# Three small moves in a hybrid decoder layer: where the last hidden blocks come back to, when the queries are copied, and which weights are fetched behind the keys

## The chip, the cores and the metric

The kernel runs on one NeuronCore of a Trainium2 chip. Its engines work side by side and wait for each other by semaphores: TensorE multiplies matrices, VectorE and ScalarE work on whole tiles, GpSimd does a few small things, and SyncE issues nearly all DMA transfers, in the order in which they are written. The metric is the time of one execution on the device in microseconds (us), as a median over runs.

## What is computed

One layer for 256 tokens of width 1024, in float32:

```
h = x + 0.5 * (silu(n1 @ w_gate1) * (n1 @ w_up1)) @ w_down1        n1 = rmsnorm(x), hidden width 2816
n = rmsnorm(h);  z = n @ w_in = q | k | v | u | gv                  each 512 wide
attn = softmax(q k^T / 8, causal) v                                 8 heads of 64; 256 tokens are one block
gm   = gelu(u) * (W_s layernorm(gelu(gv)) + b_s)                    W_s lower triangular, chunks of 128 tokens
g    = sigmoid(n @ w_gate + b_gate)                                 two gates of 1024
h = h + (g[:1024] * (attn @ w_a) + g[1024:] * (gm @ w_g)) @ w_out
h = h + 0.5 * (silu(n3 @ w_gate2) * (n3 @ w_up2)) @ w_down2         n3 = rmsnorm(h)
out = rmsnorm(h)
```

## The kernel before

**Precision.** Every large product is made of three: each float32 operand is split into a high part (a cast, on ScalarE, line 205) and a low part (the difference, on VectorE, line 207), and TensorE adds high x high, high x low and low x high (lines 200 to 202). So each weight goes through SyncE's load, ScalarE's cast and VectorE's subtraction before TensorE may use it.

**Weights.** They come in units of 1 MB, in the order in which TensorE uses them, each loaded as two halves of 512 KB (line 149, tiles `raw`) into a ring of 7 buffers (`RAW`), and split into a ring of 4 units (`w`). A half is loaded as soon as VectorE has finished with the half seven before it, unless `hold[0]` stops the loads at a number of halves. Some places set `hold[0]`, so that transfers of the program's own tiles are not queued behind weights, and set it back to `None` later.

**Order.** TensorE and SyncE run in the order in which the code is written. From the first down product to the gates ScalarE and VectorE do too (`in_order`). Elsewhere a scheduler orders these two.

**Hidden blocks.** The product `silu(g)*u` of a feed-forward layer is made with tokens on the partitions, and the down product wants features there. `glu` transposes 32x32 squares on VectorE into a tile of the ring `hg` (two buffers), `leave` stores it to DRAM (`f1way`, `f2way`), `arrive` fetches it back with the squares rearranged by four DMAs (line 381, tiles `f1back`, `f2back`), and `settle` splits it into the operand (`f1h`, `f2h`). This goes in groups of four blocks of 128 features; the 22 blocks make five groups and a last one of two. `back` is a single buffer, so a fetch waits until the group before it is split. `rest()` lists what remains when the down product begins, to be done after its weight units 1, 2, 3 and so on. The ring `hg` is also used by the transposed tiles of the first down product's output (line 542).

**The middle.** After the first down product come, with the first half of the features and then with the second, the products q, k and gv; then u and v whole, then the gates. q and k are scaled by ScalarE (line 609) and transposed by VectorE (610), stored (723, 725), and fetched back in another shape (727, 730: `qback`, and the keys into `qk`). Before the scores (line 624) the queries' tile is copied once more by ScalarE (line 743). The scores go to six PSUM banks; VectorE adds the causal mask on the way out (line 631), ScalarE copies the rest (630). The spatial product (line 673) needs the layer norm of gv, whose gain and bias (`ln_g`, `ln_b`) are fetched behind the keys (731, 732). All PSUM tiles come from one ring of eight banks, so u's two banks are next used by the spatial product, and the first two score banks by v's product (line 374). `hold[0] = 2 * mv + 2` (line 578) lets the loads run up to the first of v's two weight units until the keys' fetch has been issued (line 733).

Of the kernel before, what the change touches and what calls it, by code (L numbers as in the profile page):

```python
# [10 lines left out]
F32 = mybir.dt.float32  # L11
# [7 lines left out]
P = 128  # L19
D = 1024  # L20
S = 256
# [24 lines left out]
def block_kernel(ctx, tc, t, out):  # L46
    nc = tc.nc
# [5 lines left out]
    tmp = ctx.enter_context(tc.tile_pool(name="tmp", bufs=2))  # L53
# [53 lines left out]
    def add_units(name, n):  # L107
        first = len(units)
        units.extend((name, i) for i in range(n))
        return first  # L110
# [9 lines left out]
    mu, mv = (add_units(name, 2) for name in ("u", "v"))  # L120
    mg = add_units("gate", 8)
# [9 lines left out]
    hold = [None]  # L131
# [72 lines left out]
    def split(hi, lo, src, later=False):  # L204
        nc.scalar.copy(hi, src)  # L205
        def rest():
            nc.vector.tensor_sub(lo, src, hi.bitcast(F32))  # L207
        return rest if later else rest()
# [65 lines left out]
    def down_features(i0, n_units, both_of_k, scale, gain, nT, name, free, near, behind):  # L274
# [41 lines left out]
        for rest in lows:  # L316
            rest()
# [45 lines left out]
    def chunk(i0, nT, name, c, us=range(2), ps=None, apart=1):  # L363

        if ps is None:
            ps = [bank(f"{name}_{c}{j}") for j in range(NT)]
        for u in us:
            w = unit(i0 + 2 * c + apart * u, ALONE)  # L370
            for k in range(4):
                for j in range(NT):
                    st = tuple(p[:, j * P:(j + 1) * P] for p in block_of(nT, 4 * u + k))
                    mm3(ps[j], st, (w[:, k, 0, :], w[:, k, 1, :]), u + k == 0, u == 1 and k == 3)
        return ps

    def from_way(to, way):

        squares32 = way.rearrange("(q r) a n -> r q a n", r=32)
        for a in range(4):  # L380
            nc.sync.dma_start(to[32 * a:32 * a + 32], squares32[:, :, a, :])
# [9 lines left out]
    class Hidden:  # L391
# [28 lines left out]

        def arrive(self, p):
            n = 32 * self.blocks(p)
            self.back[p] = tmp.tile([P, S // 32, n], F32, tag="back", name=f"{self.name}back{p}", bufs=1)
            from_way(self.back[p], self.way.pop(p))

        def settle(self, p):
# [9 lines left out]
        def rest(self):  # L436

            last = NC // 2
            def first():
                self.leave(NC - 1)  # L440
                self.arrive(last - 1)
            return [first, lambda: self.settle(last - 1), lambda: self.arrive(last), lambda: self.settle(last)]


    nT = alloc_T("n1", ("nA", "nB"))
# [86 lines left out]
    with in_order():  # L532
# [25 lines left out]
        last = 2 * FB - 4  # L558
        sums = [None, None]
        for i in range(FB // 2):  # L560
            w = unit(f1d + i, ALONE)
            at = range(4 * i, 4 * i + 4)
            for s, j in [(s, j) for j in range(NT) for s in at] if 4 * i == last else [(s, j) for s in at for j in range(NT)]:
                f, b = divmod(s, FB)
# [10 lines left out]
            if i == FB // 2 - 3:  # L575
                norm_parts(0)

        hold[0] = 2 * mv + 2
        psq = chunk(mq, nT2, "q", 0, [0], apart=3)
        rs2 = []  # L580
        for j in range(NT):
# [124 lines left out]
        def layer_norm(j):  # L706
            st = small.tile([P, 6], F32, tag="st", name=f"st{j}")
            nc.vector.bn_stats(st, gv[:, j, :])
            mvr = small.tile([P, 2], F32, tag="mvr", name=f"mvr{j}")
            nc.vector.bn_aggr(mvr, st)  # L710
            ve = small.tile([P, 1], F32, tag="ve", name=f"ve{j}")
            nc.vector.tensor_scalar(ve, mvr[:, 1:2], EPS, None, op0=ALU.add)
            r = small.tile([P, 1], F32, tag="lnr", name=f"lnr{j}")
            nc.gpsimd.tensor_tensor(r, ve, nhalf, op=ALU.pow)
            nc.vector.scalar_tensor_tensor(gv[:, j, :], gv[:, j, :], mvr[:, 0:1], lng, op0=ALU.subtract, op1=ALU.mult)
            nc.vector.scalar_tensor_tensor(gv[:, j, :], gv[:, j, :], r, lnb, op0=ALU.mult, op1=ALU.add)

        chunk(mq, nT2, "q", 0, [1], psq, 3)  # L720
        turn_qk(0, psq)
        chunk(mk, nT2, "k", 0, [1], psk, 3)
# [3 lines left out]
        q_back = tmp.tile([P, S // 32, P], F32, tag="back", name="qback", bufs=1)  # L726
        from_way(q_back, qk_way[0])
        qk = act.tile([P, 2, 4 * S], F32, tag="nC", name="qk")
# [6 lines left out]
        chunk(mgv, nT2, "gv", 0, [1], psgv, 3)  # L735
        for j in range(NT):
            nc.scalar.activation(gv[:, j, :], psgv[j], AF.Gelu_apprx_tanh, scale=rs2[j])
        for j in range(NT):
            layer_norm(j)
        psu = chunk(mu, nT2, "u", 0, [0])  # L740

        qT = qk[:, 0].rearrange("p (k t) -> p k t", k=4)
        nc.scalar.copy(qT.rearrange("p k (q c) -> p q k c", c=32), q_back.rearrange("p q (k c) -> p q k c", c=32))
        chunk(mu, nT2, "u", 0, [1], psu)
        for j in range(NT):
            nc.scalar.activation(ut[:, j, :], psu[j], AF.Gelu_apprx_tanh, scale=rs2[j])
# [233 lines left out]
```

## Time and profile before

| | |
|---|---|
| Median of three runs | 529.79 us (528.45 to 531.68) |
| Profiled execution | 527.75 us, its span 526.0 us |
| TensorE busy | 515.0 us (98%) |
| VectorE busy | 352.1 us (67%) |
| ScalarE busy | 264.7 us (50%) |
| DMA | 126.82 MB, mean 241 GB/s |
| Chain that ended last | 88% TensorE, 6% DMA, 2% VectorE |

The span is the time from the first to the last instruction of the profiled execution; what lies around it makes the rest of that execution's time. The chain that ended last is followed back from the last instruction, at each step to what released it. In a timeline a row is one instruction, or several alike in a row (x4), with the time it started, how long it ran, and in brackets how long its engine was idle before and what ended that. `SPq` is SyncE issuing DMAs, and the time of such a row is that of the issues, not of the transfers. Times of TensorE's instructions overlap, so its speed is read from the distance between starts.

### The profile page before, as it was taken

The numbers are of one execution on the slowest core, as the hardware profiler recorded it, in microseconds if no ns is written. First come the engines' busy times: TensorE is split into PE (matmuls) and PEld (weight loads), VectorE is DVE, ScalarE is ACT, GpSimd is POOL, SyncE is SP. The second block draws the span as 40 slices with busy tenths as digits, with TensorE's granted clock in tenths as the row PEclk, the third lists the DMA queues.
The fourth block names the chain that finished last, engine by engine and source line by source line (L and its number), as shares of the span: only waits on it lengthen the run. The fifth ranks groups of instructions, "written<-read, shape, count | busy, mean of one in ns | idle before, by whom it ended". The sixth has DMA issues, their size and how long they took to land.

```text
span 526.0 us, 6697 instructions
## 1 busy us (share of the span) xinstructions
PE 515.0 (98%) x2401; PEld 428.4 (81%) x2401; DVE 352.1 (67%) x481; ACT 264.7 (50%) x369; POOL 12.0 (2%) x25
## 2 busy tenths in 40 slices
PE   8999999999989999989999999999999999999995
PEld 6888888888868888878888898888888888888884
DVE  6886666575447565569976787987965755575424
ACT  7755354554434545558655524666444453463402
POOL 0010000000000010000000000001000000000002
PEclk9999999999999999999999999999999999999998
DMA  8998597979767955697799666738697879677302
GB/s 317 372 340 309 152 360 254 251 232 286 192 180 236 316 173 192 156 366 278 187 357 321 241 182 175 299 117 323 209 286 266 277 257 317 190 241 219 140 0 81
DMA packets 63921, 126.82 MB, mean 241 GB/s; under 512 B 11664, under 2 KB 36752, under 8 KB 63760
## 3 DMA queue, kind: packets, MB, share of 16 engines
q1 hardware_dynamic: 63600, 126.06, 74.3%
q8 instruction: 19, 0.31, 0.2%
q10 hardware_dynamic: 288, 0.33, 0.2%
q14 instruction: 14, 0.11, 0.1%
HBM read 113.26 MB, written 13.11 MB: 240 GB/s over the span
## 4 chain that ended last, share of the span: by engine, by line
PE 88%; DMA 6%; DVE 2%; SPq 1%; issue 1%; ACT 1%; POOLq 0%; DVEq 0%; POOL 0%; ACTq 0%
PE f L200 14%; PE f L201 14%; PE f L202 14%; PE acch L202 4%; PE acch L201 4%; PE acch L200 4%; PE acc L174 3%; PE g L201 3%; PE g L202 3%; PE g L200 3%; DMA f1back<-f1way 3%; PE down L202 2%; PE down L200 2%; PE down L201 2%; DMA raw<-in_v 2%; PE acc L179 1%
## 5 line engine op out<-in xcount | busy, mean ns | idle before, releaser
L207 DVE TENSOR_TENSOR w<-raw,w 128x1024 fp32r<-128x1024 f32 x180 | 211.5, 1217 | 77.7 <-ACT w L205 77.6
L205 ACT CAST w<-raw 128x1024 fp32r<-128x1024 f32 x180 | 179.7, 1049 | 103.8 <-PE f L202 48.7
L202 PE MATMUL f<-w,n 128*128 128x512 f32 x336 | 130.7, 389 | 0.0
L200 PE MATMUL f<-w,n 128*128 128x512 f32 x336 | 130.7, 389 | 0.0
L201 PE MATMUL f<-w,n 128*128 128x512 f32 x336 | 130.7, 389 | 0.0
L202 PEld LDWEIGHTS f<-w,n 128*128 128x128 f32 x336 | 63.1, 188 | 13.1
L200 PEld LDWEIGHTS f<-w,n 128*128 128x128 f32 x336 | 63.1, 188 | 13.1
L201 PEld LDWEIGHTS f<-w,n 128*128 128x128 f32 x336 | 63.1, 188 | 13.1
L200 PE MATMUL down<-w,f1h 128*128 128x512 f32 x88 | 34.3, 390 | 1.6 <-ACT f1h L205 1.6
L202 PE MATMUL down<-w,f1h 128*128 128x512 f32 x88 | 34.4, 390 | 0.0
L201 PE MATMUL down<-w,f1h 128*128 128x512 f32 x88 | 34.3, 389 | 0.0
L200 PE MATMUL acch<-w,f2h 128*128 128x512 f32 x84 | 32.7, 389 | 0.0
L201 PE MATMUL acch<-w,f2h 128*128 128x512 f32 x84 | 32.7, 389 | 0.0
L202 PE MATMUL acch<-w,f2h 128*128 128x512 f32 x84 | 32.7, 389 | 0.0
L406 ACT ACTIVATE f2s<-f,rstd 128x256 f32<-128x256 f32 x22 | 10.3, 474 | 29.0 <-PE f L202 28.8
L200 PE MATMUL g<-w,n 128*128 128x512 f32 x64 | 24.9, 389 | 0.0
L201 PE MATMUL g<-w,n 128*128 128x512 f32 x64 | 24.9, 389 | 0.0
L202 PE MATMUL g<-w,n 128*128 128x512 f32 x64 | 24.9, 389 | 0.0
L408 DVE SCALAR_TENSOR_TENSOR f2a<-f,rstd,f2s 128x256 f32<-128x256 f32 x22 | 10.3, 474 | 20.5 <-ACT f2s L406 20.5
L406 ACT ACTIVATE f1s<-f,rstd 128x256 f32<-128x256 f32 x22 | 10.3, 473 | 24.3 <-PE f L202 22.8
L200 PEld LDWEIGHTS down<-w,f1h 128*128 128x128 f32 x88 | 16.5, 188 | 5.4 <-ACT f1h L205 2.0
L202 PEld LDWEIGHTS down<-w,f1h 128*128 128x128 f32 x88 | 16.5, 188 | 3.8 <-DVE f1h L207 0.4
(181 smaller groups left out, 648.8 us busy)
## 6 DMA issues: line engine op xcount, KB each, us to landing
raw<-in_f SPq DMA_DIRECT2D x84, 512.0 KB, 5.9
raw<-in_f1d SPq DMA_DIRECT2D x22, 512.0 KB, 6.2
raw<-in_f2d SPq DMA_DIRECT2D x22, 512.0 KB, 7.0
raw<-in_gate SPq DMA_DIRECT2D x16, 512.0 KB, 6.5
raw<-in_out SPq DMA_DIRECT2D x8, 512.0 KB, 5.4
f1way<-f1t SPq DMA_DIRECT2D x11, 256.0 KB, 6.5
f2way<-f2t SPq DMA_DIRECT2D x11, 256.0 KB, 5.0
front<-in_first SPq DMA_DIRECT2D x7, 384.0 KB, 6.0
```

The source lines that it names most:

```text
L174: nc.tensor.matmul(ps, st, both.rearrange("p two n -> p (two n)"), start=first, stop=last)
L179: nc.tensor.matmul(ps[:, n:], st, both[:, 0, :], start=False, stop=False)
L200: nc.tensor.matmul(ps, sh, mh, start=first, stop=False)
L201: nc.tensor.matmul(ps, sh, ml, start=False, stop=False)
L202: nc.tensor.matmul(ps, sl, mh, start=False, stop=last)
L205: nc.scalar.copy(hi, src)
L207: nc.vector.tensor_sub(lo, src, hi.bitcast(F32))
L406: nc.scalar.activation(sg, ps[j][:, :CH], AF.Silu, scale=rs[j])
L408: nc.vector.scalar_tensor_tensor(a, ps[j][:, CH:], rs[j], sg, op0=ALU.mult, op1=ALU.mult)
```

## The change

Three edits. **First**, a group of two blocks is fetched into a tile of the ring `hg` instead of the single buffer `back`, and `rest()` fetches it in its first step, right behind the group of four before it; splitting it moves up by one step. Since both feed-forward layers use the class, it holds for both. **Second**, the copy of the queries on ScalarE is written ahead of the layer norm and of the u products, and so ahead of the casts of the weights that those ask for. **Third**, `hold[0]` is `2 * mg`, so that both of v's units are loaded before the keys' transfers and only the gates' units behind them.

```diff
--- before.py
+++ after.py
@@ -420,7 +420,9 @@
 
         def arrive(self, p):
             n = 32 * self.blocks(p)
-            self.back[p] = tmp.tile([P, S // 32, n], F32, tag="back", name=f"{self.name}back{p}", bufs=1)
+
+            beside = dict(tag="back", bufs=1) if n == P else dict(tag="hg")
+            self.back[p] = tmp.tile([P, S // 32, n], F32, name=f"{self.name}back{p}", **beside)
             from_way(self.back[p], self.way.pop(p))
 
         def settle(self, p):
@@ -439,7 +441,8 @@
             def first():
                 self.leave(NC - 1)
                 self.arrive(last - 1)
-            return [first, lambda: self.settle(last - 1), lambda: self.arrive(last), lambda: self.settle(last)]
+                self.arrive(last)
+            return [first, lambda: self.settle(last - 1), lambda: self.settle(last)]
 
 
     nT = alloc_T("n1", ("nA", "nB"))
@@ -575,7 +578,7 @@
             if i == FB // 2 - 3:
                 norm_parts(0)
 
-        hold[0] = 2 * mv + 2
+        hold[0] = 2 * mg
         psq = chunk(mq, nT2, "q", 0, [0], apart=3)
         rs2 = []
         for j in range(NT):
@@ -714,7 +717,6 @@
             nc.gpsimd.tensor_tensor(r, ve, nhalf, op=ALU.pow)
             nc.vector.scalar_tensor_tensor(gv[:, j, :], gv[:, j, :], mvr[:, 0:1], lng, op0=ALU.subtract, op1=ALU.mult)
             nc.vector.scalar_tensor_tensor(gv[:, j, :], gv[:, j, :], r, lnb, op0=ALU.mult, op1=ALU.add)
-
 
 
         chunk(mq, nT2, "q", 0, [1], psq, 3)
@@ -735,12 +737,12 @@
         chunk(mgv, nT2, "gv", 0, [1], psgv, 3)
         for j in range(NT):
             nc.scalar.activation(gv[:, j, :], psgv[j], AF.Gelu_apprx_tanh, scale=rs2[j])
+
+        qT = qk[:, 0].rearrange("p (k t) -> p k t", k=4)
+        nc.scalar.copy(qT.rearrange("p k (q c) -> p q k c", c=32), q_back.rearrange("p q (k c) -> p q k c", c=32))
         for j in range(NT):
             layer_norm(j)
         psu = chunk(mu, nT2, "u", 0, [0])
-
-        qT = qk[:, 0].rearrange("p (k t) -> p k t", k=4)
-        nc.scalar.copy(qT.rearrange("p k (q c) -> p q k c", c=32), q_back.rearrange("p q (k c) -> p q k c", c=32))
         chunk(mu, nT2, "u", 0, [1], psu)
         for j in range(NT):
             nc.scalar.activation(ut[:, j, :], psu[j], AF.Gelu_apprx_tanh, scale=rs2[j])
```

SyncE at the start of the first down product (`raw` from `in_f1d` are its weights, `f1way` the stored hidden blocks), before:

```order
L419 DMA f1way_1207<-f1t_1145 128x2x256
L381 DMA f1back_1209<-f1way_1056 32x8x128 x4
L149 DMA raw_1_1217<-in_f1d 128x1024
L149 DMA raw_0_1221<-in_f1d 128x1024
L149 DMA raw_1_1252<-in_f1d 128x1024
L149 DMA raw_0_1256<-in_f1d 128x1024
L381 DMA f1back_1282<-f1way_1207 32x8x64 x4
```

and now:

```order
L419 DMA f1way_1207<-f1t_1145 128x2x256
L381 DMA f1back_1209<-f1way_1056 32x8x128 x4
L381 DMA f1back_1214<-f1way_1207 32x8x64 x4
L149 DMA raw_1_1222<-in_f1d 128x1024
L149 DMA raw_0_1226<-in_f1d 128x1024
L149 DMA raw_1_1257<-in_f1d 128x1024
L149 DMA raw_0_1261<-in_f1d 128x1024
```

The fetch of the last two blocks (32x8x64) stands directly behind that of the four before, and ahead of four weight halves instead of behind them.

ScalarE from the activation of gv on (`w_1876` and `w_1877` are v's second unit, `w_1910` is the first of the gates), before:

```order
L737 ACT_TABLE_LOAD
L737 ACTIVATE mixed<-gv_1689,rstd_1642 128x512
L737 ACTIVATE mixed<-gv_1690,rstd_1644 128x512
L205 CAST w_1876<-raw_0_1809 128x2x512
L205 CAST w_1876<-raw_1_1811 128x2x512
L743 COPY qk<-qback 128x8x4x32
L205 CAST w_1910<-raw_0_1813 128x2x512
L205 CAST w_1910<-raw_1_1815 128x2x512
```

and now:

```order
L739 ACT_TABLE_LOAD
L739 ACTIVATE mixed<-gv_1689,rstd_1642 128x512
L739 ACTIVATE mixed<-gv_1690,rstd_1644 128x512
L742 COPY qk<-qback 128x8x4x32
L205 CAST w_1877<-raw_0_1698 128x2x512
L205 CAST w_1877<-raw_1_1734 128x2x512
L205 CAST w_1910<-raw_0_1813 128x2x512
L205 CAST w_1910<-raw_1_1815 128x2x512
```

The copy has moved ahead of the two casts of v's second unit. Behind these rows both have the activation of u and the copies of the scores.

SyncE around the transposed queries and keys (`qkway` is where they are stored), before:

```order
L149 DMA raw_1_1694<-in_v 128x1024
L723 DMA qkway_1727<-mixed 128x2x512
L725 DMA qkway_1728<-mixed 128x2x512
L381 DMA qback<-qkway_1727 32x8x128 x4
L381 DMA qk<-qkway_1728 32x8x128 x4
L731 DMA mixed<-in_ln_g 128x512
L732 DMA mixed<-in_ln_b 128x512
L149 DMA raw_0_1809<-in_v 128x1024
L149 DMA raw_1_1811<-in_v 128x1024
L149 DMA raw_0_1813<-in_gate 128x1024
```

and now:

```order
L149 DMA raw_1_1694<-in_v 128x1024
L149 DMA raw_0_1698<-in_v 128x1024
L149 DMA raw_1_1734<-in_v 128x1024
L725 DMA qkway_1729<-mixed 128x2x512
L727 DMA qkway_1730<-mixed 128x2x512
L381 DMA qback<-qkway_1729 32x8x128 x4
L381 DMA qk<-qkway_1730 32x8x128 x4
L733 DMA mixed<-in_ln_g 128x512
L734 DMA mixed<-in_ln_b 128x512
L149 DMA raw_0_1813<-in_gate 128x1024
```

Both halves of v's second unit have moved from behind `ln_b` to ahead of the queries' store. VectorE's order in the middle is the same before and now: subtractions of v's first unit, layer norm, subtractions of v's second unit and of the gates' first, mask additions.

## Rows read from the trace of the kernel before

**Rows 1.** Waits of TensorE (line waiting, releaser, us in total, times, longest).

```profile
PE sc L624 <- ACT qk L743: 1.7, 1, 1.7
PE down L200 <- ACT f1h L205: 1.6, 1, 1.6
```

**Rows 2.** Timeline of TensorE around the first stop (start us, us, instruction, idle before).

```profile
151.28 0.39 PE L200 MATMUL down<-w,f1h 128*128 128x512 f32 x1
...
152.41 0.39 PE L202 MATMUL down<-w,f1h 128*128 128x512 f32 x1
154.40 0.50 PE L200 MATMUL down<-w,f1h 128*128 128x512 f32 x1 [1.60 <-ACT f1h L205]
...
158.00 0.39 PE L202 MATMUL down<-w,f1h 128*128 128x512 f32 x1
```

**Rows 3.** Timeline of ScalarE, the casts of the returning blocks.

```profile
140.00 1.05 ACT L205 CAST f1h<-f1back 128x1024 fp32r<-128x1024 f32 x1 [6.92 <-DMA f1back<-f1way]
...
153.73 0.62 ACT L205 CAST f1h<-f1back 128x512 fp32r<-128x512 f32 x1 [8.88 <-DMA f1back<-f1way]
```

**Rows 4.** Timeline of SyncE's queue in the same stretch.

```profile
129.92 0.43 SPq L419 DMA_DIRECT2D f1way<-f1t  x1
...
133.42 11.52 SPq L149 DMA_DIRECT2D raw<-in_f1d  x4
145.11 1.81 SPq L381 DMA_DIRECT2D f1back<-f1way  x4
```

**Rows 5.** DMA issues, 129.9 to 130.4 us (count, KB each, us to landing).

```profile
f1way<-f1t SPq DMA_DIRECT2D x1, 256.0 KB, 7.0
```

**Rows 6.** DMA issues of the whole span.

```profile
qk<-qkway SPq DMA_DIRECT2D x4, 128.0 KB, 3.8
...
f2back<-f2way SPq DMA_DIRECT2D x4, 64.0 KB, 2.0
```

**Rows 7.** Timeline of TensorE around the second stop.

```profile
230.76 0.39 PE L202 MATMUL u<-w,n 128*128 128x512 f32 x1
232.90 2.96 PE L624 MATMUL sc<-qk 64*128 64x128 f32 x32 [1.75 <-ACT qk L743]
235.79 2.05 PE L673 MATMUL mix<-mixed,wsT 128*128 128x128 f32 x16
237.60 0.47 PE L200 MATMUL v<-w,n 128*128 128x512 f32 x1
```

**Rows 8.** Timeline of ScalarE around the second stop.

```profile
229.63 1.05 ACT L205 CAST w<-raw 128x1024 fp32r<-128x1024 f32 x1 [8.63 <-DMA raw<-in_v]
230.85 1.05 ACT L205 CAST w<-raw 128x1024 fp32r<-128x1024 f32 x1 [0.17 <-DMA raw<-in_v]
231.81 1.04 ACT L743 COPY qk<-qback 128x1024 f32<-128x1024 f32 x1
...
234.65 1.25 ACT L746 ACTIVATE mixed<-u,rstd 128x512 f32<-128x512 f32 x2
```

**Rows 9.** Timeline of SyncE's queue ahead of the second stop.

```profile
210.95 0.38 SPq L723 DMA_DIRECT2D qkway<-mixed  x1
...
219.58 1.78 SPq L381 DMA_DIRECT2D qk<-qkway  x4
...
222.43 0.85 SPq L149 DMA_DIRECT2D raw<-in_v  x2
```

**Rows 10.** Timeline of VectorE, the window cut at 237.05 us.

```profile
205.08 2.36 DVE L207 TENSOR_TENSOR w<-raw,w 128x1024 fp32r<-128x1024 f32 x2 [1.94 <-ACT w L205]
...
228.41 0.75 DVE L716 SCALAR_TENSOR_TENSOR mixed<-mixed,lnr 128x512 f32<-128x512 f32 x1 [2.09 <-DMA mixed<-in_ln_b]
...
231.94 4.62 DVE L207 TENSOR_TENSOR w<-raw,w 128x1024 fp32r<-128x1024 f32 x4
236.48 0.68 DVE L631 TENSOR_TENSOR mixed<-sc,mask 128x512 f32<-128x512 f32 x1
```

**Rows 11.** Weight loads (line 149) from 205 to 245 us.

```profile
DMA to landing us min/median/max: 4.2/7.1/9.9
```

## The prediction

> **What bounds the kernel now.** I began with the list of TensorE's waits, because the page has TensorE busy for 98% of the span: a change can only give back what that engine loses. The list has four entries, 4.9 us together: two short ones before the first layer's products begin, and the two in [rows 1], which are the places that the change touches. The reader should see that nothing else in these 526.0 us is TensorE waiting, so the prize is small from the outset.
>
> Then I measured each of the two in TensorE's timeline, because the idle time that a wait shows and the time that it costs differ. In the first, five starts take 1.13 us (151.28 to 152.41), so a product of 512 columns costs 0.226 us. From 152.41 to 158.00 there are 15 starts, worth 3.39 us, and they took 5.59 [rows 2]: **2.20 us lost**, of which 1.60 is the wait and the rest a slow restart. In the second, the last product of u starts at 230.76, the next start was due at 230.99, and the first score starts at 232.90 [rows 7]: **1.91 us lost**.
>
> Why TensorE waits there: ScalarE. At 153.73 it was let go by the transfer of the last two blocks (f1back) [rows 3]. That transfer was issued only at 145.11 [rows 4], since its buffer is that of the four blocks before, which had to be cast and subtracted first (from 140.00 on). At 231.81 ScalarE copied the queries; the copy stood behind two casts of v's weights, which started at 229.63 and 230.85, each let go by its load (in_v) [rows 8]. Those loads were issued at 222.43, behind the keys [rows 9].
>
> **Part 1, a buffer for the last two blocks.** SyncE now issues the four small transfers of these blocks right behind the four of the blocks before. They read what the last store, issued at 129.92, writes [rows 4], and that store lands 7.0 us after its issue [rows 5]: SyncE stands still until 136.9 and has issued the four by about 138.8 (1.81 us, as at 145.11). When do they land? Nearest rows: 2.0 us after issue in the quiet second layer [rows 6], or, in this layer, 153.73 less 146.92 = 6.8 us after the last issue [rows 3, 4]. So 140.8 to 145.6; I take the later, since the DMA queue here is as full as there. ScalarE, which has the blocks before (140.00 to 141.05) and two weight casts ahead of it and is free from about 143, casts at 145.6 at the latest. TensorE wants the result at 152.64, the start that was due after 152.41, and the cast takes 0.62: over 6 us to spare. The stall goes whole: **-2.20 us**.
>
> What is moved behind SyncE's new wait: the weight loads that went out from 133.42 on, four in 11.52 us [rows 4]. The first slips by 5.4 us, to 138.8, and lands some 7 us later, near 146. It belongs to the eighth weight unit of this product; one unit feeds TensorE for 24 products, 5.4 us, so with the sixth beginning at 152.64 the eighth is wanted at 163.5. It needs two casts and two subtractions, under 5 us: 12 us of cover, cost zero. The new buffer comes from the ring of two in which the transposed tiles lie; its next owner is a transpose in the middle of the sixth unit, later than 155, by which time the subtraction that frees it is long done. In the second layer the same move has no wait of TensorE to remove, and adds four issues (under 2 us) ahead of loads that are needed some 16 us later. Zero.
>
> **Part 2, queries' copy first, v's weights earlier.** The two loads of v leave when VectorE frees their buffers, the second after the first subtraction of the pair that starts at 205.08, so about 206.3 [rows 10]; SyncE's next issue is the queries' store at 210.95 [rows 9]. So they go out before it. The store's own time doesn't matter, because the keys' store comes later still. The last keys' transfers are issued from 219.58 to 221.36 [rows 9] and land after 3.8 us [rows 6], at 225.2; the queries' were issued before them. So the copy ends near 224 and the scores can start when u's products end, at 230.99 instead of 232.90.
>
> What is late next? The gates' weights take v's old places in the queue, so I let their first pair be cast from 229.63 to 231.90, as v's were [rows 8]. The activation of u follows: 1.25 us, until 233.15. The scores took 2.89 us (232.90 to 235.79) [rows 7], so the spatial products are reached at 233.88, and u is ready. Then v's first product. In before it starts 4.70 us after the first score [rows 7], so now at 235.69. It writes the bank of the first scores, one of eight in a ring, and needs VectorE's mask addition there to be over. VectorE's order is unchanged: layer norm (held until 228.41 by ln_b), four weight subtractions from 231.94, and only then the mask addition, 236.48 to 237.16 [rows 10]. The subtractions follow each other without a gap now, and their inputs were there in time, so having the scores 1.91 us sooner doesn't move the addition. TensorE finds a **new wait of 1.5 us**: 237.16 plus the 0.05 us between the end of the queries' copy (232.85) and the first score (232.90) gives 237.21 against 237.60: **-0.39 us** is what is left of 1.91.
>
> The trace of before doesn't show this wait, since there the addition ended 0.44 us before v's product. Its bounds: none at all (-1.91), or a wait that eats everything (0). I take the row of the addition, because VectorE is shown busy up to it.
>
> On this point the Trainium skill has a rule, page "PSUM — Partial Sum Buffer", section "PSUM bank collisions raise a hardware error": TensorE's write and VectorE's read of one bank have to be kept apart by a semaphore. By that rule the second stall gives 0.39; if products could run into a bank that is still being read it would give 1.91. The row agrees as far as it goes (the product starts after the addition's end), but it shows no waiting.
>
> **Sum.** -2.20 - 0.39 = -2.59 us. The span goes from 526.0 to 523.4, the profiled execution from 527.75 to 525.2. That execution is 2.0 us under the median of the three runs shown (529.79), so against the median: **527.2 us**.
>
> **Rivals.**
> - *Both stalls go whole.* -2.20 - 1.91 = -4.11: 525.7. It takes a mask addition 1.5 us earlier. For it: VectorE sat 2.09 us waiting for ln_b [rows 10], and two loads of 512 KB fewer follow it. Against: ln_b is issued ahead of every one of these loads, before and now, with as many transfers in front of it. Chance 0.15.
> - *The first stall only changes its reason.* The four small transfers land after about 151.7, or ScalarE, which casts in order, waits for them and holds weights that TensorE wants. Then only 0.39 is saved: 529.4. Against: they would have to take 13 us from the last issue, twice the slowest row. The variant that the buffer isn't free falls with it: the transposed tile that lay there is stored before the first four blocks can be fetched at all. Chance 0.08.
> - *Slower: the gates' weights block ScalarE.* Their casts stand before the activation of u, and the spatial products and VectorE's subtractions wait for both. The slowest weight load in this stretch took 9.9 us [rows 11]; issued at 222.90, the second would land at 232.8, the activation would end at about 235.1 and the spatial products would start at 235.2, still no later than 235.79. From the landing to v's product it is one cast, the activation and the 1.81 us of spatial products (235.79 to 237.60), 4.1 in all, so beyond 10.2 us each us costs one, and from about 12.7 us on the whole gain is eaten. A landing at 14 us gives 531.1. Against: v's loads in the same two places needed 7 to 8. Chance 0.05.
> - *The change doesn't do what it says.* The built program has all three moves, so only the ways above remain.
>
> Forecast 0.62; the other 0.10 is for what none of these names. The three runs shown differ by 3.2 us, so 1% (5.3 us) is about what can be told from no change. Faster than 524.5 needs the first rival and a low run, or something unseen: 0.09. Slower than 535.1: 0.03. Within: 0.88. The range reaches from the first rival less half the spread of the runs (525.7 - 1.6 = 524.1) to the second plus as much (529.4 + 1.6 = 531.0).
>
> **What would show each step.** In TensorE's waits, the entry on f1h and that on the copy of the queries should be gone, and a new one should stand at v's product, released by VectorE's mask addition, of about 1.5 us. SyncE should show an issue of f1back after a wait until about 136.9, then the loads from 138.8. VectorE's time from its first use of ln_b to the mask addition should stay 8.1 us (228.41 to 236.48). The prediction is wrong if v's product starts without a wait (then the addition moved, and I mis-sized part 2), if the f1h wait survives, or if a wait appears after 240 that isn't in the list of before.

## The result and the profile after

The changed kernel takes 524.75 us (median of 6 runs, 524.45 to 524.96), the kernel before, in runs beside it, 529.51 (528.45 to 531.68). The ratio is 0.9907, 95% interval 0.9888 to 0.9927: **4.8 us less**, where 2.6 were forecast. On a second chip it is 524.80 against 529.52, ratio 0.9904 (0.9877 to 0.9930). The time lies in the range given, and just within 1%.

The two profiled executions tell another size: the span went from 526.0 to 523.2 us, the executions from 527.75 to 524.89, so 2.9 us less, close to the forecast. The runs and the profiles differ by 2 us, and most of this study is about that difference.

TensorE's waits after the change (line waiting, releaser, us in total, times, longest):

```profile
PE warm L101 <- DVE zeros L98: 1.2, 1, 1.2
PE v L200 <- DVE mixed L634: 0.6, 1, 0.6
PE f L488 <- ACT n L464: 0.2, 1, 0.2
```

Both entries of [rows 1] are gone, and one has come: v's product waits for VectorE's mask addition (line 634), as forecast, but for 0.6 us instead of 1.5.

The first stop. SyncE's queue after the change:

```profile
137.72 2.05 SPq L381 DMA_DIRECT2D f1back<-f1way  x4
139.86 0.39 SPq L149 DMA_DIRECT2D raw<-in_f1d  x1
```

The transfers of the last two blocks go out 7.4 us earlier than in [rows 4], behind a wait for the store. ScalarE's cast of them:

```profile
142.83 0.62 ACT L205 CAST f1h<-f1back 128x512 fp32r<-128x512 f32 x1
```

It carries no idle time, so it waited for nothing but its turn; in [rows 3] ScalarE had idled 8.88 us for the transfer. The cast is over some nine us before TensorE wants the operand, and the 2.20 us are gone whole.

The second stop. TensorE's timeline (start us, us, instruction, idle before):

```profile
228.91 0.39 PE L202 MATMUL u<-w,n 128*128 128x512 f32 x1
229.23 2.89 PE L627 MATMUL sc<-qk 64*128 64x128 f32 x32
232.05 2.05 PE L676 MATMUL mix<-mixed,wsT 128*128 128x128 f32 x16
234.69 0.50 PE L200 MATMUL v<-w,n 128*128 128x512 f32 x1 [0.59 <-DVE mixed L634]
```

After 228.91 the next start was due at 229.14, so 0.09 us are lost at the scores. From the first score to v it takes 5.46 us, where [rows 7] have 4.70: 0.76 lost. So the second part gives 1.91 - 0.09 - 0.76 = 1.06 us instead of 0.39. VectorE in the same stretch:

```profile
224.72 0.75 DVE L718 SCALAR_TENSOR_TENSOR mixed<-mixed,mvr 128x512 f32<-128x512 f32 x1 [5.12 <-DMA mixed<-in_ln_g]
225.89 0.75 DVE L719 SCALAR_TENSOR_TENSOR mixed<-mixed,lnr 128x512 f32<-128x512 f32 x1 [0.42 <-DMA mixed<-in_ln_b]
...
229.41 4.63 DVE L207 TENSOR_TENSOR w<-raw,w 128x1024 fp32r<-128x1024 f32 x4
233.95 1.28 DVE L634 TENSOR_TENSOR mixed<-sc,mask 128x512 f32<-128x512 f32 x2
```

From ln_b to the mask addition it is 8.06 us, forecast 8.1. But ln_b itself came sooner: 3.02 us before the last product of u, 2.35 before it in [rows 7, 10]. VectorE waits for both constants, first for ln_g and then for ln_b. In the profile of before the wait for ln_g was shorter:

```profile
225.57 0.75 DVE L715 SCALAR_TENSOR_TENSOR mixed<-mixed,mvr 128x512 f32<-128x512 f32 x1 [4.12 <-DMA mixed<-in_ln_g]
```

So part of the drop in the wait for ln_b, from 2.09 to 0.42 us, is time that VectorE now spends waiting for ln_g.

With these, the profiles add up: -2.20 - 1.06 = -3.26, and the first product of the down projection starts 0.34 us later in the profile of after (125.78 against 125.44), since this execution began more slowly. That is -2.92, and the spans differ by -2.85.

### The profile page after: what moved, and what is told of

The parts are those of the page before. It is cut to its first block, busy times and chain, and to the rows that moved or that the text cites. A ratio compares the mean times of both kernels' runs of the same rounds, so it can differ in the third digit from the quotient of the medians.

```text
span 523.2 us, 6694 instructions
## 1 busy us (share of the span) xinstructions
PE 515.1 (98%) x2401; PEld 429.1 (82%) x2401; DVE 352.1 (67%) x481; ACT 265.0 (51%) x369; POOL 12.0 (2%) x25
## 4 chain that ended last, share of the span: by engine, by line
PE 93%; DMA 3%; DVE 1%; issue 1%; ACT 1%; SPq 1%; POOLq 0%; DVEq 0%; POOL 0%; ACTq 0%
PE f L202 15%; PE f L201 15%; PE f L200 15%; PE down L202 4%; PE down L201 4%; PE down L200 4%; PE acch L202 4%; PE acch L200 4%; PE acch L201 4%; PE acc L174 3%; PE g L200 3%; PE g L202 3%; PE g L201 3%; PE acc L179 1%; DMA raw<-in_gate 1%; PE f L488 1%
```

## Experiments

Theory 1, formed after the result: a stop costs more than its length. In part of the executions TensorE's granted clock falls to half after a stop, and the one profile of before holds no such fall. Its rivals: the two profiles happened to lie off their medians, or one of the moves gives something that TensorE's waits don't list.

Some tables below divide runs by their mean granted clock over the span, which each run records. In the profiled executions without a fall in mid-span it is 0.996 to 0.999; half clock that costs 1.7 us of 528 takes 0.003 from it.

**The kernel before, profiled again** (no edit).

> The kernel before, unchanged, profiled once more. The changed kernel came out 4.8 us faster by the medians, but only 2.9 us by the two profiled spans. Theory A (the two stops vary): the stops on f1h and on the queries' copy end with a transfer's landing, and the first profile caught a short one, so the spans of these executions spread over about 3 us, from 526 to 530, and a longer span has a longer stop at one of the two places. Theory B (the clock): the stops are as long as in the first profile, but in some executions the granted clock falls after one, and the mean clock of those is visibly lower (0.99 or less against 0.997). Theory C (the start): the spread sits before the first layer's products, and both kernels have it.

Time 529.49 (ratio 1.0004, 0.9987 to 1.0022). The profile is another than the first; its execution took 529.96 us, its span was 528.1. TensorE around the second stop:

```profile
230.41 0.39 PE L202 MATMUL u<-w,n 128*128 128x512 f32 x1
233.33 4.63 PE L624 MATMUL sc<-qk 64*128 64x128 f32 x32 [2.54 <-ACT qk L743]
237.89 2.05 PE L673 MATMUL mix<-mixed,wsT 128*128 128x128 f32 x16
239.70 0.48 PE L200 MATMUL v<-w,n 128*128 128x512 f32 x1
```

The same 32 scores take 4.56 us until the spatial products, 2.89 in [rows 7]: 1.67 us lost behind the stop, not in it. The table by stretches says why (per engine its busy us and instructions; then PEclk, the granted clock as a share of full, DMA's share, GB/s):

```profile
230.00:233.00 3.00, 0.79 (x4) 0.33 (x2) 2.53 (x5) 2.77 (x3) 0.98 (x1) 1.00 1.02 418
233.00:237.00 4.00, 3.67 (x28) 3.67 (x30) 4.00 (x5) 3.69 (x7) 0.00 (x0) 0.62 0.99 382
237.00:240.00 3.00, 3.00 (x25) 2.64 (x22) 2.59 (x7) 2.36 (x6) 0.00 (x0) 0.94 1.01 385
```

The same stretch in the first profile of before:

```profile
233.00:237.00 4.00, 4.00 (x42) 3.67 (x43) 4.00 (x5) 4.00 (x9) 0.00 (x0) 1.00 1.04 393
```

PEclk is 0.62 and 0.94 here, 1.00 there. A mean of 0.62 between the two levels of 2.4 and 1.2 GHz means part of the stretch at half: 0.38 x 4 + 0.06 x 3 = 1.70 us of full-speed work lost, which is the 1.67 of the scores. Before the fall TensorE had stood still for 2.54 us. Stretches of half a microsecond show when the clock fell:

```profile
232.50:233.00 0.50, 0.00 (x0) 0.00 (x0) 0.50 (x1) 0.50 (x1) 0.00 (x0) 1.00 0.99 401
233.50:234.00 0.50, 0.50 (x10) 0.50 (x12) 0.50 (x1) 0.50 (x1) 0.00 (x0) 0.92 1.06 426
234.00:234.50 0.50, 0.50 (x10) 0.50 (x8) 0.50 (x2) 0.50 (x2) 0.00 (x0) 0.50 1.05 410
```

The granted clock is still full in the stop itself (1.00). It falls to half (0.50) at about 234.0, some 0.6 us after the scores have begun. The Trainium skill, page "TensorE: Matmul & The Clock Gate", section "HAM oscillation — how this bites in real kernels", describes this as a pattern: TensorE waits for data, its clock is throttled meanwhile, and the work after the wait starts cold. The trace agrees that the work behind the wait runs at half clock, here for a loss of 1.7 us; it does not show the clock throttled during the wait, nor cold from the first product on.

**Two more profiles of before** (no edit; one execution each).

> The kernel before once more, for its profile. Theory 1 (the stops vary and the clock falls in about half of the executions): the stop on f1h between 1.2 and 2.3 us, the one at the scores between 1.7 and 2.7; if the granted clock falls to half somewhere after 230, about 1.7 us more are lost there. Rival (one profile was typical, the other a mishap): 1.6 and 1.7 us within 0.2, and no fall.

> The kernel before once more, for its profile. The same two expectations as for the one ahead of it: by theory 1 stops of other lengths and a fall of the clock in one of the two, by the rival 1.6 and 1.7 us within 0.2 and no fall.

They took 528.07 and 527.06 us. The waits of the first:

```profile
PE sc L624 <- ACT qk L743: 1.8, 1, 1.8
PE down L200 <- ACT f1h L205: 1.3, 1, 1.3
```

and of the second:

```profile
PE sc L624 <- ACT qk L743: 1.4, 1, 1.4
...
PE down L200 <- ACT f1h L205: 1.0, 1, 1.0
```

Neither has a fall in mid-span. So over four profiles of one kernel the first stop is 1.6, 1.2, 1.3 and 1.0 us, the second 1.7, 2.5, 1.8 and 1.4: the lengths vary (the second by 1.1 us, its end set by a landing), and the one fall follows the longest. My expectation of a fall in one of these two missed.

**The own buffer alone.**

```diff
-            self.back[p] = tmp.tile([P, S // 32, n], F32, tag="back", name=f"{self.name}back{p}", bufs=1)
+            beside = dict(tag="back", bufs=1) if n == P else dict(tag="hg")
+            self.back[p] = tmp.tile([P, S // 32, n], F32, name=f"{self.name}back{p}", **beside)
...
+                self.arrive(last)
-            return [first, lambda: self.settle(last - 1), lambda: self.arrive(last), lambda: self.settle(last)]
+            return [first, lambda: self.settle(last - 1), lambda: self.settle(last)]
```

> Only the buffer for the last two blocks and their earlier fetch; queries' copy and the loads of v as before. The step of the prediction: -2.2 us (527.3), with the stop on the queries' copy left as it was (1.75 us). Theory A with the first stop as the varying one: -3.5 to -4.2 us and a spread of times under 1 us. Theory A with the second stop varying: -2.2 us and a spread that stays near 3 us.

525.64, ratio 0.9946 (0.9921 to 0.9971): 2.9 us less by the ratio, 4.0 by the medians. The eight runs lie in two groups, 525.27 to 525.71 and 527.60 to 527.97, with nothing between; two of the upper three have a mean clock of 0.993, the third 0.996. In its profile only the wait at the scores is left of the two stops (1.7 us), and the span is 523.8, so 2.2 us under the first profile of before: what the prediction's step says. The 4.0 us of the medians hold more than that step, and the spread is not under 1 us as the first form of theory A had it.

**The two moves for the queries, without the buffer.**

```diff
-        hold[0] = 2 * mv + 2
+        hold[0] = 2 * mg
...
+        qT = qk[:, 0].rearrange("p (k t) -> p k t", k=4)
+        nc.scalar.copy(qT.rearrange("p k (q c) -> p q k c", c=32), q_back.rearrange("p q (k c) -> p q k c", c=32))
         for j in range(NT):
             layer_norm(j)
         psu = chunk(mu, nT2, "u", 0, [0])
-        qT = qk[:, 0].rearrange("p (k t) -> p k t", k=4)
-        nc.scalar.copy(qT.rearrange("p k (q c) -> p q k c", c=32), q_back.rearrange("p q (k c) -> p q k c", c=32))
```

> Only the queries' copy ahead of the casts and v's second unit loaded ahead of the keys; the last two blocks come back as before. The step of the prediction: -0.4 us (529.1), since v's product then waits 1.5 us for the mask addition. From the changed kernel's profile, where that wait was 0.6 us: -1.1 us (528.4). Theory A with the first stop varying: the spread stays near 3 us, the stop on f1h is 1.6 us or more. With the second stop varying: -2.5 us and a spread under 1 us.

527.22, ratio 0.9976 (0.9954 to 0.9998): 1.3 us less by the ratio, 2.4 by the medians. Its profile has a span of 524.9, 1.1 us under the first of before; with the 2.2 of the buffer that makes the 3.3 of both. The twelve runs lie in two groups: seven at 526.57 to 527.27 with clock 0.997 to 0.999, five at 528.87 to 529.33 with clock 0.993 to 0.995. The stop at the scores is gone, so the second group most likely comes from the first stop, which this kernel keeps (1.4 us in its profile, against 0.7 at v's product). No run of the second group was profiled, and the one profile has no fall.

**v's weights earlier, alone** (`hold[0] = 2 * mg` and nothing else).

> The kernel before with the third edit alone: v's second unit is loaded ahead of the queries' store, and the copy of the queries stays behind the casts of that unit. If the loads are what the copy waits for, the casts run as soon as ScalarE comes to them (about 221 to 223), the copy follows by 225, and the scores are on time: the same as the second and third edits together, two groups of times at about 526.8 and 529.0 (the second where the clock falls after the stop on f1h), and the order of copy and casts is worth nothing. If the order matters too, the stop on the queries' copy stays at over 0.5 us.

527.26, ratio 0.9959 (0.9930 to 0.9988): by the medians the same as with the copy moved too, on another chip and with a wider spread (524.99 to 529.63). Its profile has no stop at the queries' copy:

```profile
PE down L200 <- ACT f1h L205: 2.3, 1, 2.3
...
PE v L200 <- DVE mixed L631: 0.6, 1, 0.6
```

With v's loads ahead, the casts that stand before the copy are no longer late, so the order of copy and casts gives nothing that could be measured.

**The queries' copy first, alone.**

The diff of the two moves for the queries, without its first two lines (those on `hold[0]`).

> The queries' copy ahead of the weights' casts alone; v's loads stay behind the keys. Theory 1 (the copy only passes the stop on): the scores start on time, but the casts of v and behind them u's activation are as late as before, so TensorE stops at the spatial products or at v instead, by about as much: 529 to 530, ratio 0.998 to 1.002. Rival (order on ScalarE was the whole of the second stop): the stop at the scores goes and none takes its place but 0.6 us at v, 527.3, as with both moves together.

528.57 against 528.46, ratio 0.9997 (0.9969 to 1.0025): nothing. The scores start on time, and the spatial products stop instead, as its waits show:

```profile
PE down L200 <- ACT f1h L205: 2.9, 1, 2.9
...
PE mix L673 <- ACT mixed L746: 1.2, 1, 1.2
```

v's casts still come when the loads let them, and u's activation stands behind them:

```profile
233.18 1.05 ACT L205 CAST w<-raw 128x1024 fp32r<-128x1024 f32 x1 [6.27 <-DMA raw<-in_v]
```

This profile also has a fall, at the other stop. TensorE:

```profile
153.06 0.39 PE L202 MATMUL down<-w,f1h 128*128 128x512 f32 x1
156.35 0.50 PE L200 MATMUL down<-w,f1h 128*128 128x512 f32 x1 [2.90 <-ACT f1h L205]
156.68 0.40 PE L201 MATMUL down<-w,f1h 128*128 128x512 f32 x1
157.07 0.73 PE L202 MATMUL down<-w,f1h 128*128 128x512 f32 x1
157.60 0.63 PE L200 MATMUL down<-w,f1h 128*128 128x512 f32 x1
158.03 0.63 PE L201 MATMUL down<-w,f1h 128*128 128x512 f32 x1
```

and the stretches:

```profile
154.00:157.00 3.00, 0.65 (x2) 0.30 (x2) 0.67 (x1) 1.32 (x2) 0.00 (x0) 1.00 0.46 159
157.00:161.00 4.00, 4.00 (x11) 3.11 (x11) 3.74 (x5) 3.08 (x4) 0.00 (x0) 0.57 0.34 92
```

After 2.90 us of standing still, and 0.8 us of work at full clock, the starts come 0.43 us apart instead of 0.23, and by the granted clock (1 - 0.57) x 4 = 1.72 us are lost. So both stops can bring a fall, of the same size.

**Zero products in both stops** (before, with 16 products of zeros ahead of each; their results are not used).

```diff
+            if i == 5:
+                fill = bank("fill")
+                for n in range(16):
+                    nc.tensor.matmul(fill[:, :S], zeros[:, :P], zeros, start=True, stop=True)
...
+                for i in range(16 if j == 0 else 0):
+                    nc.tensor.matmul(pair[0][:, :S], zeros[:, :P], zeros, start=True, stop=True)
```

> The kernel before with both stops left in place, and 16 products of zeros (128x256, into banks that nothing reads) written ahead of each of the two waiting instructions, so that TensorE isn't idle while it waits. In the second profile of the kernel before, the granted clock was half for 3.4 us after the stop on the queries' copy, and the scores took 4.6 us instead of 2.9. Clock theory: without idle time the clock never falls, so the slow group of times goes and the fast one stays where it was, about 527.8 (between 526.5 and 528.5, none above 529), 1.8 us under the median of before. Theory of the varying stops: the times spread as before, 526 to 531.5, with a median of 529.6 or a little more.

529.15, ratio 0.9987 (0.9969 to 1.0005): the gain that theory 1 wanted did not come. All twelve runs have a clock of 0.996 to 0.999, so the falls are gone. But the median is 1.2 us above that of the 36 runs of before with such a clock (527.96, counted below), so the filling seems to cost about what the falls cost. At the first stop the profile shows it:

```profile
152.51 0.39 PE L202 MATMUL down<-w,f1h 128*128 128x512 f32 x1
152.74 1.92 PE L566 MATMUL fill<-zeros 128*128 128x256 bf16 x16
154.87 0.50 PE L200 MATMUL down<-w,f1h 128*128 128x512 f32 x1 [0.21 <-ACT f1h L205]
```

The next product was due at 152.74 and starts 2.13 us late, 1.92 of them the filling; in the four profiles of before it starts 1.2 to 1.8 us late. Sixteen were too many. At the scores a stop was left even behind the filling (0.8 us). In this execution SyncE took long to issue the keys' fetches:

```profile
220.01 3.32 SPq L381 DMA_DIRECT2D qk<-qkway  x4
```

In the 13 other profiles that took 1.8 us. So v's loads left 6.8 us before u's last product started, where in [rows 7, 9] it was 8.3. Why the issues took longer stays open.

**The own buffer, and 12 zero products ahead of the scores.** This is the test that the one before should have been.

```diff
+                for i in range(12 if j == 0 else 0):
+                    nc.tensor.matmul(pair[0][:, :S], zeros[:, :P], zeros, start=True, stop=True)
```

> The own buffer for the last two blocks alone, and 12 zero products ahead of the first score, in the stop that is left. They compute nothing that is used. Twelve at the 0.12 us that each took in the run with sixteen are 1.4 us, less than the shortest stop seen there (1.7 us), so they should cost nothing themselves. Theory 1 (after a stop the granted clock falls to half in a part of the executions): no execution has a mean clock of 0.995 or less, the group of 527.6 to 528.0 that the own buffer alone still had is gone, all executions lie at 525.2 to 526.0, and the median stays near 525.6. Theory 2 (the two groups of times come from the length of the stop, whose end a landing sets): filling changes nothing, and both groups stay, 525.3 to 525.7 and 527.6 to 528.0.

525.34 (525.07 to 525.75), ratio 0.9936 (0.9914 to 0.9957). The clock is 0.996 or more in every run, and the upper group of the buffer alone is gone. TensorE:

```profile
228.64 0.39 PE L202 MATMUL u<-w,n 128*128 128x512 f32 x1
228.87 1.48 PE L624 MATMUL sc<-zeros 128*128 128x256 bf16 x12
230.28 2.89 PE L629 MATMUL sc<-qk 64*128 64x128 f32 x32
```

The scores still start 1.41 us after they were due; what the zeros change is that TensorE isn't idle meanwhile. This is what theory 1 asked for. In this execution the copy was over at 230.09, before the filling was (no wait is listed at the scores), so its stop would have been a short one. The evidence is that none of six runs lies in an upper group, where three of eight did. It is thin: at that rate six runs in a row would miss it 6 times in 100 by chance, and the two kernels ran on different chips. The stronger evidence on the clock is the test before: none of its twelve runs has a low mean clock, where about half of those of the kernel before had one.

**The norm's constants earlier** (the changed kernel, with ln_g and ln_b fetched ahead of the second half of q's product; run on two chips, beside the changed kernel on the second).

```diff
+        nc.sync.dma_start(lng, t["ln_g"].to_broadcast([P, GW]))
+        nc.sync.dma_start(lnb, t["ln_b"].to_broadcast([P, GW]))
         chunk(mq, nT2, "q", 0, [1], psq, 3)
...
-        nc.sync.dma_start(lng, t["ln_g"].to_broadcast([P, GW]))
-        nc.sync.dma_start(lnb, t["ln_b"].to_broadcast([P, GW]))
```

> The changed kernel with the layer norm's gain and bias fetched earlier, ahead of the second half of q, instead of behind the keys. If the new wait of v's product is there because VectorE gets to the mask addition late, and VectorE is late because it waits for the bias, then the wait of 0.6 us goes and the time falls by 0.6 us to about 524.2; VectorE should be free of the layer norm some 4 us sooner. If VectorE is bound by the casts of the gates' weights instead, the wait stays at 0.3 us or more.

> The changed kernel once more, for comparison with the next one on the same chip. Clock theory: its only stop is the 0.6 us ahead of v's product, so the times lie in one group, 524.4 to 525.2, and the granted clock shows no fall between the first product and the last.

> The changed kernel with the layer norm's gain and bias fetched ahead of the second half of q, once more. In its first profile TensorE had no wait left after the start, and the time was 523.9. Same-chip comparison: 0.6 to 0.9 us under the changed kernel, in one group of times.

523.94, ratio 0.9906 (0.9884 to 0.9928), and on the second chip 523.86, ratio 0.9886 (0.9858 to 0.9915), where the changed kernel took 524.80. That is 0.9 us less than the change, with no overlap of the runs there (523.78 to 524.04 against 524.50 to 525.04). In its profiles TensorE waits for nothing after its first products. VectorE, in that of the second chip:

```profile
224.15 3.49 DVE L207 TENSOR_TENSOR w<-raw,w 128x1024 fp32r<-128x1024 f32 x3
227.99 1.23 DVE L207 TENSOR_TENSOR w<-raw,w 128x1024 fp32r<-128x1024 f32 x1 [0.35 <-ACT w L205]
230.36 2.89 DVE L634 TENSOR_TENSOR mixed<-sc,mask 128x512 f32<-128x512 f32 x6 [1.15 <-PE sc L627]
```

and TensorE:

```profile
229.17 2.89 PE L627 MATMUL sc<-qk 64*128 64x128 f32 x32
231.99 2.05 PE L676 MATMUL mix<-mixed,wsT 128*128 128x128 f32 x16
233.80 0.47 PE L200 MATMUL v<-w,n 128*128 128x512 f32 x1
```

Now VectorE waits for the scores (1.15 us) and v starts 4.63 us after the first score. This confirms the chain of part 2 from the other end: the constants held the norm, the norm the subtractions, and these the mask addition. Both constants were moved, so it does not tell ln_b from ln_g, for which VectorE waited longer. It is the fastest of all kernels run.

## Why the prediction came out half the size

**Right: both mechanisms.** The first stop went whole, by the steps forecast: SyncE's wait until 136.9 (137.72 in fact), loads from 138.8 (139.86), a cast by 145.6 at the latest (142.83). The landing took about 2 us after the issue, as in the quiet layer [rows 6], and not 6.8, which cost nothing. No wait came out of the loads that slipped. None of the prediction's three signs of being wrong came: they watch TensorE's waits, and the larger error isn't one of them. At the second stop the copy and v's loads came in time, and the wait on the mask addition took the place of the old one.

**Wrong, the larger part: the sum's last step**, "That execution is 2.0 us under the median of the three runs shown (529.79), so against the median". I carried that difference over unchanged, as if it belonged to every execution of either kernel. It belongs to the stops, which the change takes away. Of the 75 runs of before that went beside the experiments and in the repeat of it, 39 have a mean clock of 0.995 or less, median 530.0, and 36 one of 0.996 or more, median 527.96. My profile (527.75) was one of the second kind. Of the changed kernel's 12 runs, and of the 12 with the constants earlier, none is of the first kind. A change that takes the stops away takes the falls with them: 39/75 x 2.04 = 1.06 us of the mean, and about 1.4 of the median (529.4 over all of them, against 527.96). Not all of the 2.04 is the clock: a fall measured 1.7, and the rest would be that it follows longer stops.

In numbers: from 527.96 to 524.80 (median of the 12) is -3.2 without falls, where the two profiles gave -3.26 for the two stops; the falls make it -4.6 against the median of all 75, close to the -4.8 of the first comparison. I had priced the clock at nothing: one profile showed none fall, and I didn't ask whether the next would. The spread of 3.2 us over three runs was in view; I took it as noise of the measurement, and the changed kernel, whose runs lie within 0.6 us (524.45 to 525.04), shows that the spread was the kernel's own.

**Wrong, the smaller part: the new wait of 1.5 us**, measured 0.6 (0.8 in the second profile of the changed kernel). The chain from ln_b to the addition was right (8.06 us, forecast 8.1). The step that failed is "ln_b is issued ahead of every one of these loads, before and now, with as many transfers in front of it", by which it had to land as late as before. So the addition came sooner, as the first rival had it, by 0.67 of the 1.5 us that it asked for. Whether v's earlier loads did it is likely and not shown: ln_b was issued as long before u's last product as in the profile of before (8.9 us in both), and landed 5.7 us after its issue instead of 6.4. In the four profiles with v's loads earlier that leave ln_b where it was, that time is 5.7 to 6.0 us. In the eight without it is 6.0 to 6.8 in six, but 5.5 and 5.8 in the two runs with zero products. The landing varies by itself, and I had taken it from one execution, as I had the stops.

**Not shown:** which stop had the fall in a given run without a profile, and what decides whether a stop brings one. In the profiles the fall followed stops of 2.5 and 2.9 us; one of 2.3 us, in the run with v's weights earlier alone, had none. A mean clock also holds the half clock of the program's last microseconds, so single runs may be counted to the wrong group: 0.999 less the 0.003 of a fall is 0.996. The 13 runs of before at 0.996 have a median of 528.9, which may mean that some of them hold a fall, and one of the three upper runs of the buffer alone lies there. The groups rest on the two falls seen in profiles, and on their going with the stops or with their filling.

## What to carry to other kernels

Before you add the median's distance to a profile's sum, ask what it is made of: look at the mean clock of each run, and profile the kernel before more than once, since one execution shows one length of each stop. A stop of TensorE costs its length, and in some executions a fall of the clock behind it as well; a kernel whose runs spread while its stops end on landings has a part of the spread to win. And if a wait depends on a chain (landing, norm, subtractions, mask), move its first link: fetching two small constants 18 us earlier gave 0.9 us.

## What the hardware showed that I had not expected

- A stop of 2.54 us, and one of 2.90, was followed by granted clocks of 0.62 and 0.57 over four microseconds, worth 1.7 us each; stops of 1.0 to 1.8 us, and one of 2.3, were not. In both the clock was full during the stop and fell 0.6 to 0.8 us after TensorE had work again.
- Products of zeros, which compute nothing, are enough to keep the clock: none of the 18 runs with them in every longer stop has a mean clock under 0.996.
- Small transfers of 64 KB landed 2.2 us after their issue (median of the four at 137.72) when they were issued ahead of the weight loads, where the same four, issued behind them, had needed 7.3 (6.3 to 7.3 in the eight profiles that issue them there). The 6.8 us of the prediction count from the last issue.
